# Mixture of experts in a one-core kernel: tokens gathered for two pairs of experts at once, outputs scattered by two fp32r products with a 0/1 matrix

## The chip, the cores and the metric

The kernel runs on one core of one Trainium2 chip. The metric is the device time of one execution in microseconds (us), as a median of several runs. Weights and inputs lie in HBM and come in by DMA; the core's engines are TensorE (PE, products; PEld is its weight load), VectorE (DVE), ScalarE (ACT), GpSimd (POOL) and SyncE (SP), whose queue here issues the DMAs of the weights.

## What is computed

Two transformer blocks over 256 tokens of width 1024. The second block has two layers, and each ends in a mixture of 32 experts; that part is touched. From the reference, shortened:

```python
h = layer_norm(DEEPNORM_ALPHA * h + mix, ln1_g[i], ln1_b[i])
ffn = hierarchical_moe(h, ...)          # 4 groups of 8 experts, the best group, its best 2 experts per token
h = layer_norm(DEEPNORM_ALPHA * h + ffn, ln2_g[i], ln2_b[i])

# per expert e, on the tokens that chose it
y = (silu(xb @ w_gate[e]) * (xb @ w_up[e])) @ w_down[e]      # 1024 -> 512 -> 1024
out = zeros.at[row_tok].add(y * row_gate[:, None])
```

DEEPNORM_ALPHA is 4 ** 0.25. All data are fp32.

## The kernel before

The first block, the mixers of the second block's two layers and the two expert stages follow each other. The change lies in the expert stage, the function moe, which runs once per layer.

**Router.** norm(hk, hk) normalises the tokens (hk: tokens on partitions, [128, 2, 1024]; tt is the half of 128 tokens). TensorE transposes hk, multiplies by the router's weights, and VectorE finds each token's two experts. pm holds for each token and expert the token's place among that expert's tokens (from 1; 0 if it isn't one), gt its gate. Meanwhile GpSimd applies the norm's gain and bias to hk (rows) and puts 4 ** 0.25 times hk into acc, the sum of outputs.

**Experts in pairs, 16 pairs, 64 token slots each.** An expert's weights are six slots of 1 MB (gate, up and down, two halves each), so a pair needs 12 and a layer 192. For each pair:
- gather makes a 0/1 matrix oh from pm and multiplies hk by it (fp32, 16 products of 128 columns, each two records in the trace), which puts the pair's tokens into xs with dims on partitions.
- expert_pair multiplies by gate and up. The two experts sit in the two column halves of TensorE's array ("128\*64" in the profile, 64x512 in the rows of the order), and their products run beside each other. then() gathers for the next pair. After the silu and four transposes come the down products into a PSUM tile big, eviction to y, and the scatter: y, [128 slots, 512], is multiplied by the transposed gated matrix gs (fp32, a full-array product of 512 columns, two records) for each half of the tokens and each half of the width, and VectorE adds the result to acc.

After the 16 pairs there is a loop for experts with more than 64 tokens, whose count comes from the data, and then the layer's last norm reads acc.

**Order.** The program is recorded engine by engine by a scheduler that orders instructions by a timeline of its own, so the products of neighbouring pairs and the DMAs stand interleaved; each engine then goes through its list in order. The weights' DMAs are all issued from SP's queue. RINGS names the buffer that each slot of weights takes; before, a ring of 22 (b0 to b4, d0 to d8, three buffers of a, c0 to c3, e0), gone through again and again. A DMA into a buffer waits until the products on its last content are done. Most of the ring is filled during the end of the mixer and the router.

Of the kernel before, what the change touches and what calls it, by code (L numbers as in the profile page):

```python
# [68 lines left out]
def _consts():  # L69
    c = {}  # L70
# [3 lines left out]
    # 512-point DFT at odd multiples of half a step, f and 255 - f from even and odd rows; the  # L74
    # kernel's rows are its taps 0..255 and then 511..256, whose sign such a DFT turns around
# [12 lines left out]
    par = lambda x: x.reshape(128, 2, -1).transpose(1, 0, 2)        # even rows, then odd ones  # L88
# [5 lines left out]
    # masks [source, target] of the levels of the halving tree: forward, and both directions  # L94
# [10 lines left out]
    rows = np.arange(12)[None] * 128 + p[:, None]            # slot (expert, matrix, half) of a pair  # L105
# [9 lines left out]
def _layout(inp):  # L115
    """Every device input, from the reference's inputs by layout alone."""
# [95 lines left out]
# ---------------------------------------------------------------- kernel body  # L212
# [4 lines left out]
def body(tc, I, out, dump=None, stop=99):  # L217
# [11 lines left out]
    with es:  # L229
# [37 lines left out]
        def wsplit(t, pool=0):  # L267
            """The two exact parts of a slot of weights, in halves of 1024 columns."""
# [26 lines left out]
        # ---- modulation vectors  # L295
# [37 lines left out]
        # ---- sums over d (partitions and chunks), tokens along the free axis; four chunks at a  # L333
        # time on column tiles, whose 32 equal rows the second product adds up and spreads
# [16 lines left out]
        # ---- rms  # L351
# [67 lines left out]
        # ---- hyena filters: taps, their L1 norm and their spectrum, kept in DRAM  # L419
# [65 lines left out]
        # ---- first block: half ffn on the latent and context tokens  # L485
# [30 lines left out]
        # ---- token mixers of the first block  # L516
        with ExitStack() as e1:
# [3 lines left out]
            # lower bounds: softmax over the two rows of logits, first one  # L521
# [13 lines left out]
            vt = mix.tile([128, 4, 512], F32, name="vt")       # v, tokens on partitions  # L535
# [34 lines left out]
            # forget gates of both directions, and the context's final states  # L570
            for c in range(2, 6):
# [13 lines left out]
                # context: decay from each token to the end of its direction  # L585
# [28 lines left out]
            # scores [source, target] by halving: each pair of tokens meets at one level,  # L614
            # where both decay to the reference point between the two halves
# [51 lines left out]
            # ---- hyena inputs: short convolution along the tokens  # L667
# [11 lines left out]
            # output gate of the recurrent branch  # L679
# [7 lines left out]
            # rms over each head, gate  # L687
# [16 lines left out]
            # ---- hyena: two gated long convolutions by the DFT  # L704
# [8 lines left out]
            for od in range(2):  # L713
# [8 lines left out]
                # real and imaginary parts at f and at 255 - f  # L722
# [37 lines left out]
            # the recurrent branch's part of the merge  # L760
# [14 lines left out]
            # ---- merge, output projection, residual  # L775
# [3 lines left out]
            hk = hpool.tile([128, 2, 1024], F32, name="hk")      # later the residual, tokens on partitions  # L779
# [42 lines left out]
        # ---- second half ffn, final rms, the layer norm before the second block  # L822
        with ExitStack() as e1:
# [6 lines left out]
            # x = r h w with r the rms norm's scale; centered, x - mean = r (h w - c)  # L830
# [27 lines left out]
        # ================================================================ second block  # L858
# [23 lines left out]
        def norm(x, o, gb=None):  # L882
            """(x - mean) over the standard deviation, with a gain and a bias or without, to o; tokens on partitions."""
# [20 lines left out]
        # the rings that the experts' weights go through, in the order in which the slots come free  # L904
        RINGS = ("d8 a b0 b1 b2 b3 d7 d6 d5 b4 d4 d3 d2 d1 d0 a a c0 c1 c2 c3 e0").split()
# [4 lines left out]
        def slot_tile(rs, n):  # L910
            return rs[n].tile([128, 2048], F32, name="w" + n)

        def mixer(l, hT, rwfree, last):
            """hT: layer 0's input, dims on partitions, to be scaled by its norm (F); rwfree() closes its pool."""
# [81 lines left out]
            # the second norm's gain and bias go into the router's weights and bias  # L996
# [14 lines left out]
            # ---------------- rwkv  # L1011
# [18 lines left out]
            def g_rw():  # L1030
# [26 lines left out]
                # decay sums relative to the middle of each half of the tokens  # L1057
# [15 lines left out]
                # normalised key, scaled key  # L1073
# [20 lines left out]
                # pair products inside each half of the tokens: [source, (A, P | B, Q)]  # L1094
# [13 lines left out]
                # tokens on partitions: values, and the first half's keys  # L1108
# [7 lines left out]
                # inverse of the unit triangular matrices by doubling: the two blocks of 64 tokens on  # L1116
                # the diagonal of each (tm, and tmt transposed), then the block between them
# [50 lines left out]
                # the state passes from the first half of the tokens to the second  # L1168
# [44 lines left out]
                # group norm over each head, bonus, gate  # L1213
# [23 lines left out]
            # ---------------- ssd  # L1237
# [8 lines left out]
            def g_dt():  # L1246
                # time steps: softplus, decay sums
# [109 lines left out]
            # ---------------- gla  # L1357
# [112 lines left out]
            def rw_done():  # L1470
                """The recurrence's memory turns to the sums and to the first of the experts' weights."""
# [3 lines left out]
                if l:  # L1475
                    # the first layer's last gain and bias, for the residual
# [17 lines left out]
            # ---- output projection and residual, tokens on partitions  # L1494
# [19 lines left out]
        def moe(l, mes, rings, acc, rows, wrg, rb):  # L1514
            rings.update(slots(mes, "c", 4))
# [3 lines left out]
            # ---- router  # L1519
# [4 lines left out]
            for tt in range(2):  # L1524
                xT = (mpa, rt)[tt].tile([128, 8, 128], F32, name="xs_")
# [24 lines left out]
            def first_max(x, shape, w, name):  # L1550
                """The largest along the last axis, and a one at the first place that has it."""
# [31 lines left out]
            def gates():  # L1583
# [40 lines left out]
            i4 = lambda x: x.unsqueeze(3).to_broadcast([128, 2, 2, 64])  # L1624
            f1 = lambda x: x.rearrange("p e c -> p (e c)")
# [194 lines left out]
```

## Time and profile before

| | us |
|---|---|
| time, median of 3 runs | 2489.71 (2488.13 to 2491.46) |
| span of the profiled execution, from its first to its last instruction | 2490.8 |
| first expert product to last norm, layer 0 (1244.13 to 1738.50) | 494.4 |
| first expert product to last norm, layer 1 (1980.93 to 2478.86) | 497.9 |

The profiled execution has no time of its own beside its span; the span stands 1.1 us above the median of the three runs, inside their spread. Times in the trace are counted from the span's start. Busy time of TensorE is modelled from pipelined products, so its share says only that it was never long without one.

### The profile page before, as it was taken

How to read it: one execution, taken by the hardware profiler on the slowest of the kernel's cores; microseconds unless marked ns; L12 is line 12 of the kernel's file. 1: busy time of each engine (PE TensorE's matmuls, PEld its weight loads, DVE VectorE, ACT ScalarE, POOL GpSimd, SP SyncE). 2: the span in 40 equal slices, each digit the busy share in tenths (PEclk: the TensorE clock that was granted, in tenths of full speed). 3: DMA queues.
4: the chain of work that ended last, by engine and by line, in shares of the span. 5: the costliest groups of instructions: out<-in, count | busy, mean ns of one | idle time of the engine just before them, and what ended most of it. 6: DMA issues, size and time to landing. Idle time of an engine off the chain costs nothing. (4 is left out here: it accounts for less than half of the span.)

```text
span 2490.8 us, 33000 instructions
## 1 busy us (share of the span) xinstructions
PE 2327.8 (93%) x13596; PEld 1536.9 (62%) x13596; DVE 1103.4 (44%) x1854; ACT 638.9 (26%) x975; POOL 360.2 (14%) x289
## 2 busy tenths in 40 slices
PE   8999999797998999799899999998898899999997
PEld 2667888597888999586744443333795744433332
DVE  5433554648687666665511212112865411211112
ACT  3221222345554444552200000001642200000000
POOL 1000000137542000341300000000432300000000
PEclk9999999899999999898899999999896899999999
DMA  8674223222364542333799999991334799999991
GB/s 336 257 282 157 89 98 116 85 102 85 112 223 148 186 172 103 123 118 121 304 387 419 420 419 411 401 399 66 104 113 157 289 421 419 420 406 407 388 371 35
DMA packets 87676, 602.02 MB, mean 242 GB/s; under 512 B 9665, under 2 KB 13601, under 8 KB 16161
## 3 DMA queue, kind: packets, MB, share of 16 engines
q1 hardware_dynamic: 86160, 596.98, 61.1%
q8 instruction: 110, 1.80, 0.3%
q0 software_dynamic: 576, 2.10, 0.2%
q10 hardware_dynamic: 784, 0.76, 0.1%
q14 instruction: 46, 0.37, 0.0%
HBM read 593.51 MB, written 6.29 MB: 241 GB/s over the span
## 5 line engine op out<-in xcount | busy, mean ns | idle before, releaser
L274 ACT ACTIVATE whi<-w 128x1024 fp32r<-128x1024 f32 x196 | 204.4, 1056 | 480.0 <-PE pd L285 138.5
L276 DVE TENSOR_TENSOR wlo<-w,whi 128x1024 fp32r<-128x1024 f32 (+1 forms) x196 | 219.3, 1131 | 110.4 <-ACT whi L274 109.8
L284 PE MATMUL pg<-ahi,whi 128*128 128x256 f32 (+1 forms) x704 | 231.8, 329 | 13.0 <-DVE u L677 3.9
L285 PE MATMUL pg<-alo,whi 128*128 128x256 f32 (+1 forms) x704 | 228.3, 324 | 1.4 <-DVE alo L379 1.4
L286 PE MATMUL pg<-ahi,wlo 128*128 128x256 f32 (+1 forms) x704 | 226.8, 325 | 0.2 <-DVE wlo L276 0.2
L416 DVE SCALAR_TENSOR_TENSOR hT<-pd,mg,hT 128x256 f32<-128x256 f32 x264 | 117.0, 479 | 167.2 <-PE pd L286 167.2
L1688 DVE TENSOR_TENSOR acc<-acc,pd 128x512 f32<-128x512 f32 x128 | 88.1, 688 | 226.5 <-PE pd L1687 226.5
L284 PEld LDWEIGHTS pg<-ahi,whi 128*128 128x128 f32 x704 | 136.0, 193 | 31.6 <-ACT whi L274 6.7
L285 PEld LDWEIGHTS pg<-alo,whi 128*128 128x128 f32 x704 | 135.9, 193 | 14.4 <-issue 2.8
L286 PEld LDWEIGHTS pg<-ahi,wlo 128*128 128x128 f32 x704 | 135.2, 193 | 13.3 <-issue 3.7
L278 POOL TENSOR_TENSOR wlo<-w,whi 128x512 fp32r<-128x512 f32 x64 | 108.3, 1696 | 196.3 <-ACT whi L274 154.0
L965 POOL TENSOR_TENSOR wlo<-wa,whi 128x384 fp32r<-128x384 f32 x64 | 96.0, 1505 | 258.7 <-ACT whi L963 232.1
L284 PE MATMUL pg<-ah,whi 128*128 128x256 f32 x352 | 108.0, 308 | 19.7 <-ACT whi L963 6.0
L284 PE MATMUL pu<-ahi,whi 128*128 128x512 f32 (+1 forms) x352 | 119.9, 341 | 0.2 <-ACT sq L480 0.2
L285 PE MATMUL pd<-hl,whi 128*128 128x512 f32 (+1 forms) x352 | 118.9, 339 | 1.2 <-DVE hl L409 1.2
L286 PE MATMUL pu<-ahi,wlo 128*128 128x512 f32 (+1 forms) x352 | 119.2, 339 | 0.0
L285 PE MATMUL pu<-alo,whi 128*128 128x512 f32 (+1 forms) x352 | 119.0, 338 | 0.0
L284 PE MATMUL pd<-hh,whi 128*128 128x512 f32 (+1 forms) x352 | 117.6, 342 | 1.3 <-DVE hT L416 0.9
L286 PE MATMUL pd<-hh,wlo 128*128 128x512 f32 (+1 forms) x352 | 118.6, 339 | 0.0
L285 PE MATMUL pg<-al,whi 128*128 128x256 f32 x352 | 105.2, 299 | 3.6 <-POOL al L955 3.6
L286 PE MATMUL pg<-ah,wlo 128*128 128x256 f32 x352 | 104.7, 298 | 0.0
L284 PEld LDWEIGHTS pg<-ah,whi 128*128 128x128 f32 x352 | 72.2, 206 | 26.1 <-ACT whi L963 6.9
(1643 smaller groups left out, 4852.3 us busy)
## 6 DMA issues: line engine op xcount, KB each, us to landing
wd<-in_moe_dram SPq DMA_DIRECT2D x162, 1024.0 KB, 9.5
wb<-in_moe_dram SPq DMA_DIRECT2D x90, 1024.0 KB, 9.4
w<-in_ffn_dram SPq DMA_DIRECT2D x66, 1024.0 KB, 4.8
wc<-in_moe_dram SPq DMA_DIRECT2D x64, 1024.0 KB, 10.1
wa<-in_moe_dram SPq DMA_DIRECT2D x52, 1024.0 KB, 10.2
w<-in_mod_w_dram SPq DMA_DIRECT2D x36, 1024.0 KB, 6.9
w<-in_w_in_dram SPq DMA_DIRECT2D x24, 1024.0 KB, 4.9
wa<-in_w_in_dram SPq DMA_DIRECT2D x24, 1024.0 KB, 4.8
```

What stands on the lines that cost most here:

```text
L274: S.activation(hi, c, AF.Copy)
L276: V.tensor_sub(lo[:, :n], c[:, :n], hi[:, :n].bitcast(F32))
L278: G.tensor_sub(lo[:, n:], c[:, n:], hi[:, n:].bitcast(F32))
L284: PE.matmul(o, wh, xh, start=first, stop=False)
L285: PE.matmul(o, wh, xl, start=False, stop=False)
L286: PE.matmul(o, wl, xh, start=False, stop=last)
L416: V.scalar_tensor_tensor(hT[:, dt, c], p[:, c], mg[:, dt, i:i + 1], hT[:, dt, c], op0=OP.mult, op1=OP.add)
L965: e.tensor_tensor(lo[:, x], c[:, x], hi[:, x].bitcast(F32), op=OP.subtract)
L1688: V.tensor_add(acc[:, tt, cs_], acc[:, tt, cs_], p_)
```

## The change

- The normalised tokens are split once per layer into two fp32r parts, kh and kl, before the norm's gain and bias. gather multiplies both parts, as fp32r, by a 0/1 matrix of 256 columns for two pairs of experts (32 products, one record each), and the gain and bias go in when the result is evicted, in pieces of 256 columns, one on ScalarE and one on VectorE in turn. It is called for every second pair.
- The scatter's matrix sl is 0/1 in fp32r; the gate becomes one number per slot (gs, a sum over the transposed gated matrix), applied when the down products are evicted. The gated output goes into two fp32r parts, yh (ScalarE) and yl (VectorE, which reads yh), and each half of tokens takes two fp32r products that add up in PSUM.
- The first addition to acc brings 4 ** 0.25 times hk with it; GpSimd's pass is gone.
- The ring has 19 slots (c1 to c3 are gone), and hk's own buffer joins it as a twentieth, h, from the second round on, once the first pair's additions have read hk. A new hk is made for the last norm.

```diff
-        RINGS = ("d8 a b0 b1 b2 b3 d7 d6 d5 b4 d4 d3 d2 d1 d0 a a c0 c1 c2 c3 e0").split()
+        RINGS = ("d8 a b0 b1 b2 b3 d7 d6 d5 b4 d4 d3 d2 d1 d0 a a c0 e0").split()
+        ROUND = RINGS[:12] + ["h"] + RINGS[12:]
+        ring_of = lambda i: RINGS[i] if i < len(RINGS) else ROUND[(i - len(RINGS)) % len(ROUND)]
...
+            for tt in range(2):
+                S.activation(kh[:, tt], hk[:, tt], AF.Copy)
+                V.tensor_sub(kl[:, tt], hk[:, tt], kh[:, tt].bitcast(F32))
...
-                G.tensor_scalar(acc, hk, 4 ** 0.25, None, op0=OP.mult)
...
-                for k in range(8):
-                    for tt in range(2):
-                        PE.matmul(px[:, k], hk[:, tt, 128 * k:128 * k + 128], f1(oh[:, tt]),
-                                  start=tt == 0, stop=tt == 1)
-                S.activation(xs[:, :4], px[:, :4], AF.Copy)
-                V.tensor_copy(xs[:, 4:], px[:, 4:])
+                for k0 in range(0, 8, nk):
+                    px = big().rearrange("p (k c) -> p k c", k=nk)
+                    for k in range(nk):
+                        d = slice(128 * (k0 + k), 128 * (k0 + k) + 128)
+                        for i, (x, tt) in enumerate(((kh, 0), (kl, 0), (kh, 1), (kl, 1))):
+                            PE.matmul(px[:, k], x[:, tt, d], f1(oh[:, tt]), start=i == 0, stop=i == 3)
+                    for k in range(nk):
+                        o, g_, b_ = xs[:, k0 + k, :64 * n], vcol(f"ln1_g{l}", k0 + k), vcol(f"ln1_b{l}", k0 + k)
+                        if k % 2:
+                            V.tensor_scalar(o, px[:, k], g_, b_, op0=OP.mult, op1=OP.add)
+                        else:
+                            S.activation(o, px[:, k], AF.Identity, scale=g_, bias=b_)
...
-                S.activation(gs.rearrange("p (a t) -> p a t", a=2), pt[:, :2], AF.Copy)
+                V.tensor_reduce(gs, pt[:, :2].rearrange("p a t -> p (a t)"), axis=AX.X, op=OP.add)
+                V.tensor_scalar(sl, pt[:, :2], 0.0, None, op0=OP.is_gt)
...
-                    if c:
-                        V.tensor_copy(y, p[:, cs_])
-                    else:
-                        S.activation(y, p[:, cs_], AF.Copy)
+                    S.activation(yh, p[:, cs_], AF.Copy, scale=gs)
+                    V.scalar_tensor_tensor(yl, p[:, cs_], gs, yh.bitcast(F32), op0=OP.mult, op1=OP.subtract)
                     for tt in range(2):
                         p_ = bank("pd")
-                        PE.matmul(p_, gs[:, 128 * tt:128 * tt + 128], y, start=True, stop=True)
-                        V.tensor_add(acc[:, tt, cs_], acc[:, tt, cs_], p_)
+                        PE.matmul(p_, sl[:, tt], yh, start=True, stop=False)
+                        PE.matmul(p_, sl[:, tt], yl, start=False, stop=True)
+                        if first:
+                            V.scalar_tensor_tensor(acc[:, tt, cs_], hk[:, tt, cs_], 4 ** 0.25, p_, op0=OP.mult, op1=OP.add)
+                        else:
+                            V.tensor_add(acc[:, tt, cs_], acc[:, tt, cs_], p_)
...
-            ox = gather(pm[:, :, :2])
+            ox = gather(pm[:, :, :4], 4)
```

What this does to the order of instructions is seen at three places. The mixers keep their order on all five engines.

On TensorE, the first expert products of layer 0 (L1652 before, L1667 after), right behind the first gather. wd, wa and wb are buffers of weights, xs the gathered tokens. Before:

```order
L1634 MATMUL big<-oh__10532,hk 128x128 x16
L1659 MATMUL pd<-ident,og__10593 128x128 x2
L1652 MATMUL pg<-wd_10596,xs__10551 64x512
L1652 MATMUL pg<-wa,xs__10551 64x512
L1652 MATMUL pg<-wd_10596,xs__10551 64x512
L1652 MATMUL pg<-wa,xs__10551 64x512
L1652 MATMUL pg<-wd_10596,xs__10551 64x512
L1652 MATMUL pg<-wa,xs__10551 64x512
L1652 MATMUL pg<-wd_10596,xs__10551 64x512
L1652 MATMUL pg<-wa,xs__10551 64x512
L1652 MATMUL pg<-wb_10621,xs__10551 64x512
L1652 MATMUL pg<-wb_10623,xs__10551 64x512
```

and after, from the second expert product on:

```order
L1667 MATMUL pg<-wa,xs__10531 64x512
L1667 MATMUL pg<-wb_10640,xs__10531 64x512
L1667 MATMUL pg<-wb_10642,xs__10531 64x512
L1667 MATMUL pg<-wd_10615,xs__10531 64x512
L1667 MATMUL pg<-wa,xs__10531 64x512
L1667 MATMUL pg<-wb_10640,xs__10531 64x512
L1667 MATMUL pg<-wd_10615,xs__10531 64x512
L1667 MATMUL pg<-wa,xs__10531 64x512
L1667 MATMUL pg<-wb_10642,xs__10531 64x512
L1667 MATMUL pg<-wb_10640,xs__10531 64x512
L1667 MATMUL pg<-wd_10615,xs__10531 64x512
L1667 MATMUL pg<-wa,xs__10531 64x512
```

The four products on each of the first two buffers stood in the first 8 rows; now four buffers' products are mixed, and the last product on wa is the thirteenth.

On TensorE, where the scatter of one pair stands among the gate and up products of the next (L1687 before, L1704 and L1705 after). Before, in the second pair of layer 0:

```order
L1652 MATMUL pg<-wc_10763,xs__10664 64x512
L1687 MATMUL pd<-y__10707,gs__10670 128x512 x2
L1652 MATMUL pg<-wc_10765,xs__10664 64x512
L1652 MATMUL pg<-wc_10763,xs__10664 64x512
L1652 MATMUL pg<-wc_10765,xs__10664 64x512
L1652 MATMUL pg<-wc_10763,xs__10664 64x512
L1652 MATMUL pg<-wc_10765,xs__10664 64x512
L1634 MATMUL big<-oh__10775,hk 128x128 x7
L1687 MATMUL pd<-hh__10715,gs__10670 128x512 x2
L1634 MATMUL big<-oh__10775,hk 128x128 x9
```

and after, behind the second pair's down products:

```order
L1667 MATMUL pg<-wa,xs__10784 64x512
L1704 MATMUL pd<-yh__10881,sl__10831 128x512
L1667 MATMUL pg<-wd_10933,xs__10784 64x512
L1704 MATMUL pd<-yh__10881,sl__10831 128x512
L1667 MATMUL pg<-wc_11016,xs__10784 64x512
L1705 MATMUL pd<-yl__10882,sl__10831 128x512 x2
L1667 MATMUL pg<-we_11026,xs__10784 64x512
L1667 MATMUL pg<-wd_11028,xs__10784 64x512
```

The products on yh and on yl stand apart, with 64-column products between them. Counted over the whole stage, changes between 64-column and full-array products go from 98 to 128 in layer 0 and from 104 to 124 in layer 1.

On VectorE, the end of the norm ahead of the router in layer 0 (L888 to L893 are lines of norm, xs or xT the transposed tokens, lgt the router's result, L1507 before and L1510 after the residual's last addition). Before:

```order
L1507 SCALAR_TENSOR_TENSOR hk<-hk,pd 128x256
L888 BN_STATS lnst<-hk 128x6
L889 BN_AGGR lnmv<-lnst 128x2
L1531 COPY xs__10442<-pd 128x512
L893 TENSOR_SCALAR hk<-hk,lnmv 128x1024
L1531 COPY xs__10463<-pd 128x512
L1541 TENSOR_TENSOR lgt<-pg,rb 128x72
```

and after:

```order
L1510 SCALAR_TENSOR_TENSOR hk<-hk,pd 128x256
L888 BN_STATS lnst<-hk 128x6
L889 BN_AGGR lnmv<-lnst 128x2
L1541 COPY xT<-pd 128x512
L1528 TENSOR_TENSOR kl<-hk,kh 128x1024
L893 TENSOR_SCALAR hk<-hk,lnmv 128x1024
L1528 TENSOR_TENSOR kl<-hk,kh 128x1024
L1541 COPY xT<-pd 128x512
L1551 TENSOR_TENSOR lgt<-pg,rb 128x72
```

One subtraction kl stands ahead of the second half's normalisation and one ahead of the copy that the router's products read.

## Rows read from the trace of the kernel before

**Rows 1.** Page, parts 1 and 6: busy time; DMA issues (us to landing last).

```profile
span 2490.8 us, 33000 instructions
...
PE 2327.8 (93%) x13596; PEld 1536.9 (62%) x13596; DVE 1103.4 (44%) x1854; ACT 638.9 (26%) x975; POOL 360.2 (14%) x289
...
wa<-in_moe_dram SPq DMA_DIRECT2D x52, 1024.0 KB, 10.2
```

**Rows 2.** Busy time by stretch; last three columns PEclk, DMA share, GB/s.

```profile
1244.13:1738.50 494.37, 482.61 (x2238) 202.66 (x2238) 91.45 (x142) 35.07 (x65) 9.56 (x16) 1.00 0.90 368
1980.93:2478.86 497.93, 485.06 (x2238) 203.10 (x2238) 91.47 (x143) 35.39 (x65) 9.24 (x15) 1.00 0.88 361
1258.00:1530.00 272.00, 269.89 (x1276) 118.09 (x1276) 51.59 (x81) 18.71 (x36) 5.55 (x9) 1.00 1.01 419
1530.00:1676.00 146.00, 142.08 (x663) 58.40 (x659) 27.56 (x43) 9.57 (x18) 2.47 (x4) 1.00 0.99 400
```

**Rows 3.** Waits of SP's queue, 1244.13 to 1700: total, times, longest.

```profile
SPq L1696 <- PE pg L1652: 241.5, 80, 9.5
SPq L1696 <- PE big L1676: 120.2, 27, 9.1
```

**Rows 4.** Waits of TensorE, 1244.13 to 1738.50; first and second of nine.

```profile
PE pd L1667 <- DVE hh__12600 L1664: 0.9, 1, 0.9
PE big L1676 <- DVE hh__11850 L1669: 0.8, 1, 0.8
```

**Rows 5.** Timeline of SP: first issue after a release, and the last, layer 0.

```profile
1247.81 0.33 SPq L1696 DMA_DIRECT2D wd<-in_moe_dram  x1
...
1676.07 0.33 SPq L1696 DMA_DIRECT2D wa<-in_moe_dram  x1
```

**Rows 6.** Timeline of TensorE: first product, second gather, a scatter among 64-column products.

```profile
1244.13 0.64 PE L1652 MATMUL pg<-wd,xs__10551 128*64 128x512 f32 x1 [0.47 <-ACT xs__10551 L1637]
...
1258.07 3.84 PE L1634 MATMUL big<-oh__10645,hk 128*128 128x128 f32 x32
...
1637.38 1.02 PE L1652 MATMUL pg<-wb,xs__12224 128*64 128x512 f32 x2
1638.33 1.99 PE L1687 MATMUL pd<-y__12267,gs__12230 128*128 128x512 f32 x4
1640.25 3.65 PE L1652 MATMUL pg<-wb,xs__12224 128*64 128x512 f32 x14
```

**Rows 7.** Timeline of the end of layer 0's stage.

```profile
1727.70 0.59 PE L1676 MATMUL big<-wa,hh__12608 128*64 128x512 f32 x1
1728.13 0.59 PE L1676 MATMUL big<-wd,hh__12608 128*64 128x512 f32 x1
...
1731.43 0.60 ACT L1684 ACTIVATE y__12635<-big 128x512 f32<-128x512 f32 x1 [15.74 <-PE big L1676]
...
1736.01 0.69 DVE L1688 TENSOR_TENSOR acc<-acc,pd 128x512 f32<-128x512 f32 x1 [0.17 <-PE pd L1687]
...
1738.50 2.71 DVE L888 BATCH_NORM_STATS2 lnst<-acc 128x6 f32<-128x256 f32 x8 [1.80 <-DMA wa<-in_wa_dram]
```

**Rows 8.** Timeline of TensorE in the first block: fp32r products of 512 and 256 columns.

```profile
300.02 0.39 PE L285 MATMUL pg<-alo,whi 128*128 128x512 f32 x1
300.25 0.39 PE L286 MATMUL pg<-ahi,wlo 128*128 128x512 f32 x1
...
960.23 0.28 PE L284 MATMUL pg<-ahi,whi 128*128 128x256 f32 x1
960.35 0.28 PE L285 MATMUL pg<-alo,whi 128*128 128x256 f32 x1
```

**Rows 9.** Page, part 5: busy, mean ns of one, idle before, releaser.

```profile
L274 ACT ACTIVATE whi<-w 128x1024 fp32r<-128x1024 f32 x196 | 204.4, 1056 | 480.0 <-PE pd L285 138.5
L276 DVE TENSOR_TENSOR wlo<-w,whi 128x1024 fp32r<-128x1024 f32 (+1 forms) x196 | 219.3, 1131 | 110.4 <-ACT whi L274 109.8
```

**Rows 10.** Timeline of layer 0's router on GpSimd and VectorE.

```profile
1228.58 5.45 POOL L1618 TENSOR_SCALAR acc<-hk 128x2048 f32<-128x2048 f32 x1
...
1228.97 3.42 DVE L1556 TENSOR_TENSOR e1k<-lgt,e1m 128x64 f32<-128x64 f32 x1
...
1233.75 0.22 DVE L1556 TENSOR_TENSOR e2k<-e,e2m 128x64 f32<-128x64 f32 x1
```

**Rows 11.** Busy time by stretch, layer 0's router; columns as in rows 2.

```profile
1225.00:1237.00 12.00, 3.69 (x18) 3.58 (x18) 9.23 (x34) 0.41 (x2) 8.87 (x3) 0.50 0.34 141
```

More of the change, by code (lines that the diff above doesn't have):

```diff
@@ L910, in slot_tile @@
         def slot_tile(rs, n):
-            return rs[n].tile([128, 2048], F32, name="w" + n)
+            return rs[n].tile([128, 2048], F32, name="hk" if n == "h" else "w" + n)
         def mixer(l, hT, rwfree, last):
@@ L1514, in moe @@
         def moe(l, mes, rings, acc, rows, wrg, rb):
-            rings.update(slots(mes, "c", 4))
+            nonlocal hk
+            rings.update(slots(mes, "c", 1), h=hpool)
             mpa = pool(mes, "mpa")
@@ L1518, in moe @@
             norm(hk, hk)
+            kh = mpa.tile([128, 2, 1024], F32R, name="kh")
+            kl = mpa.tile([128, 2, 1024], F32R, name="kl")
+            for tt in range(2):
+                S.activation(kh[:, tt], hk[:, tt], AF.Copy)
+                V.tensor_sub(kl[:, tt], hk[:, tt], kh[:, tt].bitcast(F32))
             rp = ExitStack()
@@ L1524, in moe @@
             for tt in range(2):
-                xT = (mpa, rt)[tt].tile([128, 8, 128], F32, name="xs_")
+                xT = rt.tile([128, 8, 128], F32, name="xT", bufs=2)
                 for q in range(2):
@@ L1617, in gates, with gather @@
                 rings.update(slots(mes, "e", 1, side="right"))
-                G.tensor_scalar(acc, hk, 4 ** 0.25, None, op0=OP.mult)
                 dump(f"gt{l}", gt)
                 dump(f"pm{l}", pm)
-            i4 = lambda x: x.unsqueeze(3).to_broadcast([128, 2, 2, 64])
+            wide = lambda x, n: x.unsqueeze(3).to_broadcast([128, 2, n, 64])
             f1 = lambda x: x.rearrange("p e c -> p (e c)")
-            def gather(slots):
-                oh = mp.tile([128, 2, 2, 64], F32, name="oh_")
-                V.tensor_tensor(oh, iota.unsqueeze(1).unsqueeze(1).to_broadcast([128, 2, 2, 64]), i4(slots), op=OP.is_equal)
-                px = big().rearrange("p (k c) -> p k c", k=8)
-                for k in range(8):
-                    for tt in range(2):
-                        PE.matmul(px[:, k], hk[:, tt, 128 * k:128 * k + 128], f1(oh[:, tt]),
-                                  start=tt == 0, stop=tt == 1)
-                xs = mpa.tile([128, 8, 128], F32, name="xs_")
-                S.activation(xs[:, :4], px[:, :4], AF.Copy)
-                V.tensor_copy(xs[:, 4:], px[:, 4:])
+            def gather(slots, n):
+                oh = mp.tile([128, 2, 4, 64], F32R, name="oh_")[:, :, :n]
+                V.tensor_tensor(oh, iota.unsqueeze(1).unsqueeze(1).to_broadcast([128, 2, n, 64]), wide(slots, n), op=OP.is_equal)
+                xs = mpa.tile([128, 8, 256], F32, name="xs_")
+                nk = 16 // n
+                for k0 in range(0, 8, nk):
[10 more added lines that the diff above has]
+                            S.activation(o, px[:, k], AF.Identity, scale=g_, bias=b_)
@@ L1639, in gather, with expert_pair @@
                 return oh, xs
-            def expert_pair(oh, xs, gate, wsl, then):
+            def expert_pair(oh, xs, gate, wsl, then, first=False):
                 og = mp.tile([128, 2, 2, 64], F32, name="og_")
-                G.tensor_tensor(og, oh, i4(gate), op=OP.mult)
+                G.tensor_tensor(og, oh.bitcast(F32), wide(gate, 2), op=OP.mult)
                 pgu = []
@@ L1659, in expert_pair @@
                     PE.transpose(pt[:, tt], f1(og[:, tt]), ident)
-                gs = mp.tile([128, 256], F32, name="gs_")
-                S.activation(gs.rearrange("p (a t) -> p a t", a=2), pt[:, :2], AF.Copy)
+                gs = mp.tile([128, 1], F32, name="gs_")
+                sl = mp.tile([128, 2, 128], F32R, name="sl_")
+                V.tensor_reduce(gs, pt[:, :2].rearrange("p a t -> p (a t)"), axis=AX.X, op=OP.add)
+                V.tensor_scalar(sl, pt[:, :2], 0.0, None, op0=OP.is_gt)
                 hh = mp2[0].tile([128, 512], F32, name="hh_")
@@ L1694, in wsl @@
                 def wsl(m, e, hf):
-                    t = slot_tile(rings, RINGS[(12 * pr + 4 * m + 2 * hf + e) % len(RINGS)])
+                    t = slot_tile(rings, ring_of(12 * pr + 4 * m + 2 * hf + e))
                     SP.dma_start(t, I["moe"][l, 2 * pr + e, m, hf])
                     return t
-                es2 = lambda pr: slice(2 * pr, 2 * pr + 2)
-                ox = expert_pair(*ox, gt[:, :, es2(pr)], wsl, lambda: pr < 15 and gather(pm[:, :, es2(pr + 1)]))
+                j, e0 = pr % 2, 2 * pr
+                more = lambda: gather(pm[:, :, e0 + 2:e0 + 6], 4) if j and pr < 15 else None
+                ox = expert_pair(ox[0][:, :, 2 * j:2 * j + 2], ox[1][:, :, 128 * j:128 * j + 128],
+                                 gt[:, :, e0:e0 + 2], wsl, more, pr == 0) or ox
             if l:
@@ L1742, in moe @@
                 one_ = lambda x: x.rearrange("p a e o -> p a (e o)")
-                expert_pair(*gather(one_(pp)), one_(gp), wsl2, lambda: None)
+                expert_pair(*gather(one_(pp), 2), one_(gp), wsl2, lambda: None)
+            hk = hpool.tile([128, 2, 1024], F32, name="hk")
             last = norm(acc, hk, rows if l else None)
```

3 lines of the change are left out of this document (2 added, 1 removed).

## The prediction

> **What bounds the kernel now.** I read the page first: TensorE is busy for 93% of the span [rows 1], a modelled share that doesn't say where a microsecond counts. The stages tell more. The two expert stages take 494.4 and 497.9 us [rows 2], 40% of the span, and only they and the router ahead of them change.
>
> In them two things are nearly full at once, and the waits tell which comes last. DMA engines are busy for 101% of 1258 to 1530 and for 99% after it, at 419 and 400 GB/s [rows 2]. But SP's queue, which issues the loads, waits 242 and 120 us for TensorE to finish with a buffer [rows 3], while TensorE never waits for a load: its list has nine waits of 0.8 or 0.9 us, all for VectorE or ScalarE [rows 4]. So the products set the pace. The loads are right behind: a slot is 1.0486 MB, which at 419 GB/s takes 2.50 us, so 12 slots take 30.0 us, and the stage's mean per pair is 494.4 / 16 = 30.9 us. Whatever is taken off TensorE can bring no more than the loads let through. The one reserve is the ring: before the first expert product 22 slots have been filled, and at the end the products work off those that are left after the loads have ended (last issue at 1676.07, some 10 us to land, last expert product ending about 1731 [rows 1, 5, 7]).
>
> **The products' sum.** Prices are spacings from start to start. Gather: 32 records took from 1258.07 to the next work 3.7 us (the row's 3.84 less the last record's tail [rows 6]); fifteen of these lie in the stage, 55 us. In their place come 7 gathers of 32 fp32r products of 256 columns at 0.12 us [rows 8], 27 us. Scatter: 64 products of two records at 0.43 us, 55 us; now 128 fp32r products of 512 columns at 0.23 us [rows 8], 29 us. Against this stand more changes between 64-column and full-array products. The pair of records at 1637.38 is followed after 0.95 us, where the records alone take 0.43, and the four of the scatter take 1.92 instead of 1.72 [rows 6]: a change there and back costs 0.7 us. Layer 0 gets 30 changes more by the order's count, 15 there and back, 11 us. So 494.4 - 55 + 27 - 55 + 29 + 11 = 451 us for layer 0, 43 less; layer 1, with 20 more changes, 497.9 - 54 + 7 = 451.
>
> **The loads' sum.** From the first expert product: the first release comes with the thirteenth row of the order instead of the eighth. Eight rows took 3.68 us until the next issue [rows 5, 6]; thirteen at 0.43 and one more for halves that don't alternate give 6.3 us. By then 19 slots are in, not 22, so 173 of the 192 are still to come, at 2.50 us each 433 us. Start, landing of the last and stalls: before, 170 slots (425 us) took from 1247.81 to about 1686, 13 more, and a part of that is the slower pace after 1530 that the products set; I take 7. From the first product on the last slot to the norm took 10.8 us (1727.70 to 1738.50 [rows 7]), and the new way there has the same four additions on VectorE and two evictions ahead of them, so I keep it. Together 6.3 + 433 + 7 + 10.8 = 457 us, a little above the products' 451. The last of the loads becomes the bound; the products run out of landed slots only near the end. Gain: 494.4 - 457 = 37 in layer 0, 497.9 - 457 = 41 in layer 1.
>
> **The router.** kh and kl come in ahead of the experts. A half takes 1.06 us on ScalarE and 1.13 on VectorE, as the same split of weights does [rows 9], and VectorE, in order, has one kl ahead of the second half's normalisation and one ahead of the copy that the router's products read. Fully exposed that is 2 x 2.2 = 4.4 us per layer; fully hidden behind the norm's small ScalarE steps and the transposes, nothing. In the other direction, GpSimd's pass over hk goes, and in layer 0 a VectorE instruction that takes 0.22 us took 3.42 beside it [rows 10]; GpSimd's gain and bias still run there, later by as much as kl, so the same may happen beside them. The first gather has as many columns to stream as before. I take 2 us per layer, with 0 and 4.4 as ends.
>
> **What lies beside other work.** VectorE is busy for 91 of 494 us in the stage, ScalarE for 35 [rows 2]. New per pair on VectorE are two yl, the sum and the mask, and two of the gather's pieces net of the copy they replace; none has more columns than an addition of 0.69 us [rows 7], so at most 6 x 0.69 = 4 us of a pair's 28. ScalarE gets less. That costs nothing by busy time; if the scheduler's order leaves a link of the chain (yh, then yl, then the product) exposed, it costs TensorE that link, 0.6 to 0.7 us. The buffer h can be filled once the first pair's additions have read hk; the order has its first load behind twenty others after the first release, 20 x 2.50 = 50 us in; ahead of the last product of the first pair's scatter stand 86 half-array products (37 us), half a gather (2), eight scatter products (2) and some changes, about 45 us in all, so no load waits.
>
> **Sum.** 37 + 41 - 2 x 2 = 74 us off the profiled span of 2490.8, 2417; the median of the runs stands 1.1 us lower, so 2416.
>
> A rule that would change the answer is in the Trainium skill, DMA: Bandwidth & Descriptors, section Specifications: it puts the fabric's ceiling at 435 GB/s and the HBM limit of a core at about 358. By 435 a slot would take 2.41 us (an estimate from that page), the loads' sum would be 441 and the products would stay the bound at 451. By 358 it would be 2.93 us and the stage 531, longer than before. The trace has 419 over 272 us, which rules the lower figure out here and leaves the higher open.
>
> **Rivals.**
> - *The loads go faster than 419 GB/s and the products still set the pace.* 419 is what was moved while SP waited for buffers. For it: buffers will be free earlier, so more loads are queued. Against it: DMA engines are at 101% in that stretch, with no gaps to fill. The stage is then 451: 43 + 47 - 4 = 86 us off, 2404.
> - *New waits on TensorE take the place of the fp32 passes.* The scatter now needs yl, which needs yh; the products on yh and yl stand apart, with gate and up products between, and TensorE can't pass a waiting one. For it: such waits already exist at 0.8 us [rows 4]. Against: they are nine in a stage. Two more per pair make 2 x 16 x 0.8 = 26 us per layer, the products' sum 477, the gain 17 + 21 - 4 = 34, 2456. With both links of both halves exposed (2 x 1.3 us per pair, 41 per layer) the sum is 492 and the gain 4, which is within 0.2%: the change then does nothing.
> - *The clock falls, and the kernel gets slower.* Once TensorE waits for loads, its granted clock may go down: in the router it was at 0.50, the lower level of 1.2 GHz, with TensorE busy for 3.7 of 12 us [rows 11]; in the stage it is 1.00 [rows 2]. At that level a pair's 27 us of products become 54, 27 more. The gain of 74 is used up by 74 / 27 = 2.7 pairs of the 32 at the lower level; with two pairs at the end of each layer it is 4 x 27 = 108 and the time 2416 + 108 = 2524. Against it: by the two sums TensorE lacks some 6 us of loads per layer, all at the end, and slow products let the loads catch up.
>
> The Trainium skill, TensorE: Matmul & The Clock Gate, section HAM oscillation, describes this very course, a kernel whose TensorE waits for DMA in each step and starts each step at half rate. No row here shows it inside an expert stage.
>
> **How the numbers follow.** The load-bound case at 2416: 0.55. Its own range comes from the ends above: router 0 to 4.4 per layer (-4 to +5), stalls 3 to 13 instead of 7 (-8 to +12), so 2404 to 2433. Faster loads at 2404, down to 2396 with a free router: 0.15. New waits, 2433 to 2484: 0.22; waits that eat all of it: 0.03. A slower clock: 0.05. The range leaves out the last two and the upper part of the new waits, 2396 to 2450. 0.2% is 5 us, about what a measurement of this kernel can tell from no change. Faster by more: 0.55 + 0.15 + 0.22 = 0.92; within: 0.03; slower: 0.05.
>
> **What would show it.** Each stage, from first expert product to norm, about 457 us. DMA at about 419 GB/s from some 8 us after the first product to some 12 us before the norm, without the 400 of the second stretch. Landing times of loads grow from 10 us to over 20, since buffers come free ahead of the loads. SP's waits for TensorE shrink; TensorE's own list shows waits for DMA in the last two or three pairs only. Gathers of about 3.8 us, seven in a stage; scatter products 0.23 us apart. First expert product about 2 us later in layer 0. It is wrong if TensorE waits for VectorE or ScalarE by tens of us per stage, if DMA idles in the stage's first half (a release that comes late in SP's order), or if the granted clock in the stage is below 1.

## The result: 47 us faster, and the profile after

The median is 2443.6 us against 2490.6 of the kernel before: ratio 0.9825, 95% interval 0.9807 to 0.9844. 74 us were forecast. The profiled execution has 2443.39 us, its span is 49.3 us shorter.

| us | before | after | difference |
|---|---|---|---|
| start to the norm's last aggregate ahead of layer 0's router | 1218.4 | 1212.5 | -5.9 |
| from there to the first expert product | 25.8 | 25.0 | -0.8 |
| stage, layer 0 | 494.4 | 474.7 | -19.6 |
| its norm to layer 1's first expert product | 242.4 | 241.4 | -1.0 |
| stage, layer 1 | 497.9 | 476.4 | -21.5 |

I don't put the first line down to the change: the code up to there is the same, and in the runs below that point lies between 1212.0 and 1224.5 us, at 1213.9 in the one that changes the ring alone. That leaves 43 us for the change in these two executions, where 74 had been forecast; all that is missing is in the two stages.

Page of the kernel after: busy time, and one kind of DMA issue (the last number is the landing time).

```profile
span 2441.5 us, 32095 instructions
PE 2252.4 (92%) x13084; PEld 1477.6 (61%) x13084; DVE 1157.6 (47%) x1970; ACT 674.3 (28%) x1011; POOL 354.1 (15%) x287
...
wa<-in_moe_dram SPq DMA_DIRECT2D x56, 1024.0 KB, 19.9
```

The stages by stretch, columns as in [rows 2]:

```profile
1237.44:1712.17 474.73, 446.46 (x1983) 173.69 (x1982) 117.62 (x197) 50.61 (x81) 9.54 (x16) 1.00 0.94 389
1953.61:2430.02 476.41, 448.76 (x1983) 173.72 (x1982) 117.62 (x197) 50.57 (x80) 9.23 (x15) 1.00 0.93 384
1258.00:1530.00 272.00, 259.01 (x1169) 102.79 (x1170) 70.94 (x119) 30.07 (x49) 5.54 (x9) 1.00 1.01 420
1530.00:1676.00 146.00, 137.95 (x605) 52.48 (x602) 33.76 (x58) 13.68 (x22) 3.08 (x5) 1.00 1.01 420
```

Against [rows 2], TensorE's busy time fell by 36 us, but its idle time rose from 11.8 (494.37 - 482.61) to 28.3. In both stretches the loads now run at 420 GB/s. These are waits of TensorE in 1237 to 1707 (total, times, longest):

```profile
PE pd L1704 <- DVE acc L1709: 3.8, 6, 0.6
PE pd L1685 <- DVE hh__11514 L1682: 0.9, 1, 0.9
PE pd L1704 <- ACT yh__12791 L1700: 0.9, 1, 0.9
...
PE big L1694 <- ACT xs__11346 L1653: 0.8, 1, 0.8
...
PE big L1694 <- DVE hh__11803 L1687: 0.8, 1, 0.8
```

The whole list has no DMA and adds up to 23.6 us. It has waits of the scatter for the additions (six, 3.8 us) and for yh (two, 1.7 us), of the transposes of hh for silu times up (eight, 6.9 us, in the pairs that have no gather behind their up products any more; before, one), and of the down products for the gather's last piece (five, 4.0 us; before, none) or for the copy of the transposed hh (eight, 6.4 us; before too). Before, there were ten waits of 0.8 or 0.9 us ([rows 4] and the prediction say nine) and four shorter ones, 9.5 us together. SP, which had waited for TensorE [rows 3], now mostly waits for its own earlier loads:

```profile
SPq L1717 <- DMA wd<-in_moe_dram: 143.3, 70, 2.3
SPq L1717 <- DMA wb<-in_moe_dram: 80.2, 39, 2.1
...
SPq L1717 <- PE pg L1667: 27.7, 20, 9.7
```

The end of the stage, from SP's, TensorE's and VectorE's timelines:

```profile
1660.40 0.33 SPq L1717 DMA_DIRECT2D hk<-in_moe_dram  x1
...
1700.51 0.59 PE L1694 MATMUL big<-hk,hh__12764 128*64 128x512 f32 x1
...
1712.17 2.71 DVE L888 BATCH_NORM_STATS2 lnst<-acc 128x6 f32<-128x256 f32 x8 [2.06 <-DMA wa<-in_wa_dram]
```

The last load, into the buffer h (named hk here), lands at about 1660.4 + 19.9 = 1680.3, and TensorE comes to it 20 us later. So the products were last, not the loads.

### The profile page after: what moved, and what is told of

The parts are those of the page before. It is cut to its first block, busy times and chain, and to the rows that moved or that the text cites. A ratio compares the mean times of both kernels' runs of the same rounds, so it can differ in the third digit from the quotient of the medians.

```text
span 2441.5 us, 32095 instructions
## 1 busy us (share of the span) xinstructions
PE 2252.4 (92%) x13084; PEld 1477.6 (61%) x13084; DVE 1157.6 (47%) x1970; ACT 674.3 (28%) x1011; POOL 354.1 (15%) x287
## 5 line engine op out<-in xcount | busy, mean ns | idle before, releaser
L1709 DVE TENSOR_TENSOR acc<-acc,pd 128x512 f32<-128x512 f32 x120 | 77.1, 684 | 140.7 <-PE pd L1705 140.7
## 6 DMA issues: line engine op xcount, KB each, us to landing
wd<-in_moe_dram SPq DMA_DIRECT2D x174, 1024.0 KB, 19.9
wb<-in_moe_dram SPq DMA_DIRECT2D x100, 1024.0 KB, 19.9
wa<-in_moe_dram SPq DMA_DIRECT2D x56, 1024.0 KB, 19.9
wc<-in_moe_dram SPq DMA_DIRECT2D x18, 1024.0 KB, 19.9
```

The lines of the kernel that those rows point to most:

```text
L1709: V.tensor_add(acc[:, tt, cs_], acc[:, tt, cs_], p_)
```

## The experiments

Theory P, formed from this: TensorE sets the pace by its own list with its new waits. Theory L, the forecast's: the loads do. Stage lengths (layer 0, layer 1) are from the first expert product to the norm, as above. The diffs are shortened, and the kernels of the runs have them in full. Runs given without an interval are single executions. An interruption is a place where full-array products stand between two groups of 64-column products.

**Half the loads.**

```diff
-SP.dma_start(t, I["moe"][l, 2 * pr + e, m, hf])
+SP.dma_start(t[:, :1024], I["moe"][l, 2 * pr + e, m, hf][:, :1024])
```

> The changed kernel, in which only the first half of the columns of every expert weight slot is loaded and the products read that half twice (so half of the experts' weights is left out of the result). Every product, eviction and wait stays where it is; the loads' bytes in the expert stages are halved. Theory P (TensorE sets the pace: 446 us of products and 24 us of new waits for VectorE and ScalarE, the loads are no bound): the stage of layer 0, first expert product to the norm, stays at 475 us, within 4. Theory L (the loads at 419 GB/s set the pace, TensorE's short waits only absorb what it would have waited for weights): the waits of 0.8 us shrink and the stage falls to 460 us or less.

461.4 and 459.4, about L's number. But the scheduler orders the instructions by a model of their times, loads included: TensorE's list came out differently (73 groups of 64-column products instead of 64), so the 13 us can't be put down to the loads, and the expectation's "stays where it is" was wrong. The run is made again below with a fixed list.

**No low part in the scatter.**

```diff
-V.scalar_tensor_tensor(yl, p[:, cs_], gs, yh.bitcast(F32), op0=OP.mult, op1=OP.subtract)
...
-PE.matmul(p_, sl[:, tt], yl, start=False, stop=True)
```

> The changed kernel without yl: its eviction and its product are left out, so the outputs of the experts are scattered in one fp32r pass, with less precision. Per stage TensorE loses 64 products that took 19 us, and the link yh, yl, product. Theory P: TensorE's sum falls from 471 to about 445 us, below the loads' sum of 457 that was forecast, so the stage ends at 455 to 460 us, with TensorE's first waits for loads near the end. Theory L: the loads set the pace already, only the last pair's scatter gets shorter, and the stage is 471 us or more.

452.9 and 452.7, a little below P's 455 to 460. This list is another one too (54 groups), so the 22 us are not the price of yl alone; but the loads are the same, and the stage got shorter, so they had not set its length. Here the last load lands at 1663.9 + 19.9 = 1683.8, 442.8 us after the first expert product (442.9 in the changed kernel), and TensorE's first product on it stands there: this is where the loads end a stage.

```profile
1683.82 0.64 PE L1694 MATMUL big<-hk,hh__12644 128*64 128x512 f32 x1
```

**The gather alone; the scatter alone.** In the first the scatter is the old one; the second is the kernel before with these lines in place of y and its product:

```diff
+S.activation(yh, p[:, cs_], AF.Copy, scale=gs)
+V.scalar_tensor_tensor(yl, p[:, cs_], gs, yh.bitcast(F32), op0=OP.mult, op1=OP.subtract)
...
+PE.matmul(p_, sl[:, tt], yh, start=True, stop=False)
+PE.matmul(p_, sl[:, tt], yl, start=False, stop=True)
```

> The changed kernel with the scatter of the kernel before: fp32 products with the gates in the 0/1 matrix, y copied once, two products per half. The gather for two pairs and the ring stay. Theory P: against the kernel before, the gathers' 55 us become 27 and the halves of the pairs without a gather expose silu and the multiplication (8 x 0.85 us), so the stage of layer 0 is about 473 us, as fast as the whole change: the scatter brings nothing that the waits and mode changes do not take back. The forecast's own sum (no new waits) would have 494 - 55 + 27 - 5 = 461 us.

> The kernel before with the new scatter alone (yh and yl, gates at the eviction, two fp32r products), the gather per pair in fp32 and a ring of 21 slots for want of space. Theory P: the scatter's own 60 us become 42, but gate and up products grow by 8 us around its changes of mode and the waits for yh, yl and the additions take 6 us, so the stage of layer 0 is 488 to 492 us, hardly shorter than the 494 of before. The forecast's own sum (55 us become 29, 11 us of changes) has 479 us.

Gather alone: 474.1 and 476.0, the whole at 2440.4 us (ratio 0.9793 to 0.9826), so as fast as the whole change. Scatter alone: 485.3 and 484.9, 2465.5 us (0.9888 to 0.9921), better than P expected and worse than the forecast's 479. Apart they take 20.3 and 9.1 us off layer 0, together 19.6: beside the new gather the scatter is worth nothing, in the lists that the scheduler made. With the old scatter the list has 51 groups of 64-column products, 30 of them odd in number, with the new one 64 and 50; what that costs is found below. The two scatters were not compared under one list. The gather alone, layer 0:

```profile
1237.63:1711.69 474.06, 454.62 (x1983) 173.18 (x1982) 97.02 (x149) 43.54 (x80) 9.54 (x16) 1.00 0.94 390
```

28.0 us less busy than in [rows 2], and 7.7 us more idle (474.06 - 454.62 = 19.4). Its list has seven waits of the transposes of hh for silu times up (6.3 us) and four of the down products for the gather's last piece (3.2 us), with the scatter's products of before.

**The ring alone** (the kernel before without c1, c2, c3).

> The kernel before with a ring of 19 slots in place of 22 and nothing else (the scheduler makes its lists anew). The forecast's reading: the loads had a reserve, TensorE sets the pace, and three slots fewer cost the loads 7.5 us at the start, which stay hidden, so the stage of layer 0 stays at 494 us, within 4. If the reserve of the ring already counted, it grows by up to 7.5 us to 502.

495.4 and 500.2, 1.0 and 2.2 us more than before: the reserve hid it.

**Three single waits.** A PSUM tile for each half of the down products; the transposes of the gated rows under issue_after; the gather in halves.

```diff
-p = big()
...
 for c in range(2):
+    p = big()[:, :512]
```

> The changed kernel with the down products of each half of the columns in a PSUM tile of its own, so that yh and yl of the first half can be made while the second half's products run. Theory P (TensorE sets the pace, and its new waits are those of the scatter for yh, yl and the additions): the six waits of the scatter's products (6.2 us), the part of its 42 us that is a hidden wait for yl (about 10 us) and the five waits for the gather's last piece shrink, so the stage of layer 0 falls from 474.7 to about 460 us. Theory L (loads set the pace): it stays within 3 us of 475.

```diff
 with tc.issue_after(i.ins):
     nxt = then()
+    pt = bank("pd").rearrange("p (a t) -> p a t", a=4)
+    for tt in range(2):
+        PE.transpose(pt[:, tt], f1(og[:, tt]), ident)
```

> The changed kernel with the two transposes of a pair's gated 0/1 rows issued behind the pair's last up product, beside the other full-array products, instead of between gate and up products of 64 columns. The order has 57 interruptions of the 64-column products in layer 0 in place of 64. Theory P: at 0.7 us for each there and back that is 5 us, and the transposes fill 0.3 us of the wait for silu in the eight pairs without a gather, so the stage falls from 474.7 to about 468 us. Theory L: within 3 us of 475.

```diff
-more = lambda: gather(pm[:, :, e0 + 2:e0 + 6], 4) if j and pr < 15 else None
+def more():
+    if not j:
+        nx["oh"] = mask(pm[:, :, e0 + 4:e0 + 8], 4, mp if pr % 4 else mp2[0])
+        nx["xs"] = []
+    nx["xs"].append(half(nx["oh"], 4, j))
```

> The changed kernel with the gather for two pairs cut in two: half of the rows is gathered in each pair, so that every pair has 16 products between its last up product and the transposes of hh, instead of 32 in every second pair. It needs one more half buffer, for which the ring has 18 slots instead of 19 (2.5 us more of loads after the first release). The number of interruptions in the order is the same (63). Theory P: the eight waits for silu and the multiplication, 6.8 us, and the wait for the gather's last piece go, and the stage falls to about 467 us. Theory L: it grows by the 2.5 us of the missing slot, to 477.

474.9 and 470.8, 477.5 and 474.6, 471.8 and 473.0: P missed all three. L's number came out in the first two, but not for L's reason: the last load landed over 30 us before the norm in each. In the first the waits for yh went from two to five, and those for the additions stayed. In the second the eight waits for silu shrank to 0.5 us, but the down products' waits for the gather's last piece grew from five of 0.8 to four of 1.6 us. In the third, where every pair but the last two has gather products behind its up products again, the waits for silu went from eight to two, those for the gather's last piece went, and TensorE's idle time fell from 28.3 to 22.8 us: the gather had covered them. Its busy time rose by 2.6 us, from 446.5 to 449.1. Each edit makes the scheduler's list anew.

**The first two together.**

> The changed kernel with both edits, a PSUM tile for each half of the down products and the transposes of the gated rows behind the last up product. The order has 50 interruptions in layer 0 in place of 64. Theory P: 14 interruptions at 0.7 us and about 16 us of waits go from TensorE's 471 us, so that its sum falls to about 446 us, below the loads, and the stage ends where the loads let it: 453 us by the run without yl (457 by the forecast's sum), 20 us less per layer, the whole about 2443 - 41 = 2402 us, with waits of TensorE for loads in the last pairs. Theory L: within 3 us of 475 per stage, the whole within 8 us of 2443.

459.0 and 459.6, the whole 2414.5 us (0.9685 to 0.9714): 6 us above P's 453, and without a wait for a load in TensorE's list. The idle time is what it was; the busy time fell:

```profile
1249.23:1708.25 459.02, 430.92 (x1985) 169.55 (x1984) 115.78 (x198) 51.02 (x80) 9.54 (x16) 1.00 0.97 403
```

Idle 28.1, busy 15.5 less than in the changed kernel, with the same products. So P's waits were only half of the story. The changed kernel's timeline has the price of an interruption:

```profile
1278.07 0.64 PE L1667 MATMUL pg<-wb,xs__10784 128*64 128x512 f32 x1
1278.08 0.64 PE L1667 MATMUL pg<-wd,xs__10784 128*64 128x512 f32 x1
1278.55 0.59 PE L1667 MATMUL pg<-wb,xs__10784 128*64 128x512 f32 x1
1278.56 0.59 PE L1667 MATMUL pg<-wd,xs__10784 128*64 128x512 f32 x1
1279.08 0.50 PE L1704 MATMUL pd<-yh__10718,sl__10668 128*128 128x512 f32 x1
...
1302.93 1.07 PE L1667 MATMUL pg<-wd,xs__10784 128*64 128x512 f32 x2
1303.94 0.51 PE L1704 MATMUL pd<-yh__10881,sl__10831 128*128 128x512 f32 x1
...
1699.21 0.59 PE L1694 MATMUL big<-wb,hh__12764 128*64 128x512 f32 x1
1699.64 0.59 PE L1694 MATMUL big<-wb,hh__12764 128*64 128x512 f32 x1
1700.07 0.59 PE L1694 MATMUL big<-wb,hh__12764 128*64 128x512 f32 x1
```

A 64-column product is two records of the same slot. Two of them, one for each half of the array, run side by side and take 1.01 us to the next full-array product; one alone takes 1.01 as well. Inside a group, with both halves at work, the two records of a product take 0.86 us until the next (1699.21 to 1700.07). So a group of n products takes 0.855 for each two, rounded up, and some 0.17 for the interruption. By this rule the changed kernel's list (64 groups, 50 of them with an odd number, 768 products) has 409 x 0.855 + 64 x 0.17 = 360.6 us, and the timeline, without idle time, 361.8; the list above (50 groups, 24 odd) has 347.1 and 348.6; the kernel before (49 groups, 36 odd) 352.0 and 352.8. It is no exact rule: in other lists above the timeline has up to 6 us more, in a few groups, and why is open. The Trainium skill, TensorE: Matmul & The Clock Gate, Part 3 (Packing small matmuls), says that products on different tiles of the array overlap; the rows agree (0.01 us apart) and add what a product without a partner costs.

**A list written by hand.** Every product of the stage is put behind the one before it, in whole pairs of halves (in outline):

```diff
+def pe(f, *a, **kw):
...
+            c.enter_context(tc.issue_after(chain[0].ins))
+        i = f(*a, **kw)
+    chain[:] = [i]
...
+scatter(Q, 0); gu(P, 0, 1, range(4)); scatter(Q, 1); gu(P, 1, 0, range(4)); gu(P, 1, 1, range(4))
...        # the gather in every second pair, the transposes of the gated rows
+gu(N, 0, 0, range(2)); transposes(hh); gu(N, 0, 0, range(2, 4)); down(P)
```

P is the pair, Q the one before, N the next; gu(pair, matrix, half of the rows, its four row blocks) issues gate or up products, transposes and down stand for the lines of before.

> The changed kernel with the same operations in the expert stage, but TensorE's list written by hand: the half-array products always in whole pairs of the two halves, 4 interruptions per pair and none after an odd number, the scatter of a pair in two groups that stand 8 products apart, products of the next pair's gate ahead of and behind the transposes of hh, and a PSUM tile for each half of the down products. Theory P with the loads' floor: TensorE needs 384 x 0.855 + 64 x 0.17 = 339 us for the half-array products, 27 for gathers, 36 for the scatter and 15 for transposes, with a few us of waits about 422, and the loads then set the pace. From the first expert product to the last landing took 443 us in every run so far, and about 10 us follow, so the stage is 453 us, with some 25 us of waits of TensorE for loads, mostly in the last pairs; the whole is about 2443 - 45 = 2398 us. If nothing but TensorE's own list counted, the stage would be 426 us and the whole 2345.

> The kernel with the list written by hand, in which only the first half of the columns of every expert weight slot is loaded and read twice (half of the experts' weights is left out of the result). Here TensorE's list is the same instruction by instruction, which it was not in the first run with half loads. If the loads set the stage of the hand-written list, it falls from about 453 to TensorE's own 426 us, within 6, in each layer. If it doesn't fall, TensorE sets the pace there as well and my sum for its list is wrong.

With all loads 450.7 and 450.2, and 2390.6 us in all: 0.9615 of before (0.9599 to 0.9632), the fastest here. With half of them 423.4 and 423.0. By stretch, first all loads, then half of them, layer 0:

```profile
1237.50:1688.21 450.71, 435.07 (x1985) 176.91 (x1984) 115.76 (x199) 51.12 (x81) 9.57 (x16) 1.00 0.99 410
```

```profile
1242.17:1665.53 423.36, 418.11 (x1985) 163.06 (x1984) 115.75 (x198) 51.11 (x81) 9.57 (x16) 1.00 0.67 223
```

TensorE's list is the same in both, so the 27.3 us are the loads'. With all of them TensorE waits for loads, 12 times listed, 10.4 us together, and its first product on the last slot comes as it lands (issue at 1657.81, 19.9 to land). These waits begin at 1465 us, halfway, and not in the last pairs as expected:

```profile
PE big L1718 <- DMA wd<-in_moe_dram: 3.0, 3, 1.3
PE pg L1718 <- DMA wd<-in_moe_dram: 2.1, 3, 0.8
```

```profile
1677.74 0.64 PE L1718 MATMUL big<-hk,hh__12779 128*64 128x512 f32 x1
```

The other 17.0 us lie in the busy time, all in 19 groups of 64-column products; the full-array ones take as long as with half the loads (0.06 us less in sum). In such a group one half of the array goes on while the other waits; here a load into wd lands at 1522.87:

```profile
1521.86 1.07 PE L1718 MATMUL pg<-wb,xs__11919 128*64 128x512 f32 x2
1522.92 0.64 PE L1718 MATMUL pg<-wd,xs__11919 128*64 128x512 f32 x1
```

**Odd numbers by themselves.**

```diff
-gu(N, 0, 0, range(2)); transposes(hh); gu(N, 0, 0, range(2, 4))
+gu(N, 0, 0, range(2), 1); transposes(hh); gu(N, 0, 0, range(2, 4), 2)     # 1: without the last product, 2: with it
```

> The hand-written list with half loads (half of the experts' weights is left out of the result, so that TensorE alone sets the pace), in which the four transposes of hh stand one half-array product earlier: after 3 products and ahead of 21 instead of after 4 and ahead of 20. This happens 15 times in a stage; the number of interruptions, the operations and the loads are the same. If an odd number of half-array products between two full-array ones leaves a product without a partner and costs its whole 0.855 us, the stage's 423.4 us become 423.4 + 15 x 0.855 = 436 us. If only the number of interruptions counts, as in the forecast's 0.7 us for each there and back, the stage stays at 423 us, within 2.

436.0, as the rounding up has it, all of it in the busy time. The 64-column products take 351.6 us (by the rule 399 x 0.855 + 62 x 0.17 = 351.7), and 339.0 in the run before (384 x 0.855 + 62 x 0.17 = 338.9):

```profile
1238.12:1674.14 436.02, 430.78 (x1985) 167.16 (x1984) 115.75 (x199) 51.12 (x81) 9.58 (x16) 1.00 0.66 216
```

## Why the sign was right and the size wrong

**The products' sum (451) is the step that failed.** It came out as 474.7, above the loads. Its terms, by spacings summed over layer 0's stage (without idle time; they add up to the busy times):

| term, us | forecast | measured |
|---|---|---|
| gathers | -28 | 55.11 to 27.30: -27.81 |
| scatter products | -26 | 60.48 to 42.05: -18.43 |
| interruptions (gate, up, down, transposes) | +11 | 367.02 to 377.11: +10.09 |
| idle time of TensorE | 0 | 11.76 to 28.27: +16.51 |

The four terms make -19.6, where the forecast had -43. The gather was priced rightly. The scatter's products are 0.23 us apart inside a group, but they stand in small groups, each of which takes some 0.2 us more; a group of four took 1.01 to 1.47 us instead of 0.92. The interruptions' sum was about right for the wrong reason: of its 0.7 us there and back, read at one place [rows 6], 0.43 is the half pair that a product without a partner leaves, and only the rest, 0.29, is the change of mode. The idle time, which the sum left out, is the largest part of what is missing: it was put at nothing because VectorE and ScalarE had room by busy time. The gather had covered silu in every pair, and now does so in every second. By the forecast's own sign of being wrong, tens of us of waits for VectorE and ScalarE per stage, it was wrong: 23.6.

**The rival of new waits is what happened.** It had 477 for the stage, from two waits more per pair, and the size came out nearly right with other waits. Of the link that it named, yh, yl and product, the list has three, 1.9 us; six are for the additions, and eight for silu and five for the gather's last piece are of a kind that it didn't name. That these come from the gather, which was meant to be pure gain, is shown by two runs: with the gather alone 28.0 us went off TensorE's busy time and 20.3 off the stage, and with the gather in halves the waits for silu went from eight to two and those for its last piece to none.

**The loads' sum (457) was a floor that the change did not reach.** First release 6.3 us after the first product, as forecast; last landing after 442.9 (446 forecast). The hand-written list reached it: 440.2 to the last landing, 10.5 from there to the norm (10.8 forecast), together 450.7. The 7 us for start and stalls were too much. The rival of faster loads did not come either: with buffers free ahead of the loads they moved 420 GB/s, against 419 before. The ceiling of 435 GB/s that the Trainium skill has (DMA: Bandwidth & Descriptors, Specifications) was not seen.

**Smaller steps.** The stretch at 400 GB/s is gone, landing takes 19.9 us (over 20 forecast), SP's loads wait for TensorE some 40 us instead of 362: right. TensorE's waits for loads in the last pairs: none, wrong. The router: 0.8 and 1.0 us shorter instead of 2 longer. kl took 1.22 and 2.18 us, but the second normalisation went from 2.33 to 0.81, and the instruction that took 3.42 beside GpSimd [rows 10] to 2.12. That GpSimd's smaller load did it is argued, not shown. The clock: 1.00 in both stages, and in the hand-written list, which does wait for loads, too; the rival of a slower clock did not come. Evictions on VectorE and ScalarE had room by busy time (118 and 51 of 475 us), and cost time all the same, through the order in which TensorE meets them. One slip of the sums: faster loads with a free router make 2404 - 4 = 2400, not the 2396 that became the lower end of the range.

2443.6 lies above the 2404 to 2433 of the case that was forecast. It lies in the whole range only because that took in the lower part of the new waits, which had a chance of 0.22; the reason behind 2416 did not hold.

## What to carry to other kernels

An operation that is removed may be the cover of a wait: before its time is booked as gain, look what finishes beside it, and add what is left uncovered. Where two halves of the array work side by side, count the products between interruptions; here an odd number cost as much as the next even one. When single repairs move a stage by nothing because a scheduler answers each with another list, fix the list, and compare under the same list.

## What was not expected of the hardware

- A lone half-array product costs as much as two: 30 groups with an odd number of products, where all had been even, made a stage of 423.4 us 436.0. That is 12.7 us (from the unrounded times), and 15 x 0.855 is 12.8.
- SP's loads land 19.9 us after issue, about 8 x 2.50, and the issues wait for the landing of earlier loads. By their issue and landing times eight loads are under way at nearly every issue of the changed kernel's stage, where before it was three to seven. No run here changed the limit.
- TensorE's busy time hides waits for loads: of the 27.3 us that the loads cost the hand-written list, 17.0 lie in the busy time (435.1 against 418.1), in groups where one half of the array waits for its slot and the other works on.
